# The attention's queries are turned behind the second and fourth piece of the gates in every group

## The chip, the cores and the metric

The kernel runs on one core of one Trainium2 chip. The metric is the device time of one execution in microseconds (us). Three executions of the kernel before took 1663.3 to 1664.22 us, with a median of 1663.74 us. Durations in the text come from one further execution that was profiled; it took 1663.35 us, of which 1661.6 us lie between its first and its last recorded instruction (the span).

A core has four computing engines that run side by side, each with its own queue of instructions: TensorE (PE in the profile: matrix products and transposes, with its weight loads as PEld), VectorE (DVE), ScalarE (ACT) and GpSimd (POOL). SyncE (SP) issues the DMAs that load the weights. TensorE writes its results into PSUM, which has eight banks of 128 x 512 numbers of 32 bits; ScalarE and VectorE read them from there.

## The reference

The reference is one block of a network with two branches over 256 tokens of width 2048, with 256 more tokens of context. What matters here is the attention branch:

```
xn = rmsnorm(x) * (1 + scale) + shift                     # 256 x 2048, likewise cn from the context
aq, ak, av, ag, ... = split_columns(xn @ w_in)            # w_in: 2048 x 19456
q = axial_rope(aq) * 128 ** -0.5                          # 16 heads of 128, 4 key heads
s = [q . k of the window (|i - j| <= 128), q . k of the context]
p = softmax over [s, sink]
att_branch = (p @ [v, v_ctx]) * silu(ag)
...
y = sigmoid(ma + b0) * (hg_branch @ w_o_hgrn) + sigmoid(mb + b1) * (att_branch @ w_o_attn)
out = rmsnorm(x + gate * (y @ w_out))
```

The other branch (`hg_branch`) is a gated linear recurrence in both directions. It is finished before the attention begins.

## The kernel before

All products are made from numbers split into a high and a low part (`h` and `lo`, of the type fp32r), with three matmuls for each pair of tiles (`mm3`: high x high, high x low, low x high). So each chunk of 128 x 1024 weights that a DMA has brought (`raw`) goes through ScalarE, which copies the high part (`wh`, L75), and through VectorE, which subtracts it (`wl`, L76). There are three buffers for each of `wh` and `wl` and four for `raw`. The projections write into four PSUM banks of the pool "pj"; four more banks with names of their own ("tp", "o", "al1", "al2") serve everything else.

The attention works in four groups of four heads. For group j, the generator `group_in(j, st)` makes the queries (`proj_tok_g`, eight chunks, two banks `bq`, one for each half t of the tokens) and then the gates (`proj_col_x_g`, two halves `hf` of four chunks each). A chunk of gates is called a piece in this text; it is 16 matmuls, of L140 and L145. Pieces have the numbers 0 to 7 (`4 * hf + k0 // 4`), and "step s" is the place in the program behind piece s.

A half t of the queries has two parts in `turn_q(t)`. The first is the rotation by position (`rope`, VectorE: L877, two L882, L885), from the bank into `qr`, with `rt` beside it. The second is the turn: four transposes on TensorE (L923) into `tkq`, a tile in the bank "o"; a scaled copy by ScalarE for the high part (L925); and one VectorE instruction for the low part (L926). Both write `qTa`. The table `TURNS[j][t]` says behind which step the turn of half t stands. The rope of half 0 stands ahead of piece 0, that of half 1 behind it.

When a half of the gates is finished, each of its two banks is reduced (`halves_sum`: ScalarE copies one half into `hsum`, L154, VectorE adds the other, L155); then come a sigmoid on ScalarE (L945) and a product on VectorE (L946), into `ga`. The tiles `qr`, `rt`, `hsum` and `br` (below) share two buffers, those of the tag "bb" in the pool `base`.

The generator `attend(sts)` works on 32 pairs n of a head and a half of the tokens, eight for each group. `scores(n)` makes three matmuls into the bank `sc` (L82 to L84) and then the softmax: VectorE masks, takes the maximum and its negative (L960 to L962), ScalarE takes the exponential and scales the result (L964, L965, L968), VectorE adds and inverts the sum (L966, L967). `turned(n)` transposes the probabilities of a pair (L978, `tkp`, bank "tp") and splits them (L857, L858) into `pT`. `values(m)` makes twelve matmuls for four heads into `oba`, a tile in the bank "o" (the same bank as `tkq`), and VectorE multiplies the result by the gates into `br` (L988), from which the split tiles `bH` and `bL` are made.

`alternate(attend(sts), fill(sts), 1)` weaves the two generators. `fill` runs groups 1 to 3 and then two chunks of another projection, and each `yield` of one hands over to the other. For one n the program therefore has: `scores(n)`, one chunk of `fill`, then `values(n // 4 - 1)` where n is 6, 10, 14 and so on, `turned(n - 2)`, and another chunk of `fill`. Group 0 is made before any scores, woven with the transposes of the keys.

In this part the order of TensorE's instructions is the order of the program (`tc.manual_schedule(engines={PE})`). The orders of ScalarE's, VectorE's, GpSimd's and SyncE's queues are set by a planner that simulates the program in time and gives each engine, when it comes free, the ready instruction with the highest priority; within one priority the earlier one in the program goes first. `tc.high_priority(x)` raises the priority of what is issued inside it: the splits of weights have `PRIO`, `scores`, `turned` and `values` have `2 * PRIO`, and the evictions of a turn have none.

The places of the turns, counted in `values`: in groups 1 and 3 step 3 is followed by piece 4, then by a `values` and a `turned`, and then by step 4. In group 2 it is the same: `values(2)` stands between pieces 4 and 5.

Of the kernel before, what the change touches and what calls it, by code (L numbers as in the profile page):

```python
# [7 lines left out]
F32 = mybir.dt.float32  # L8
F32R = mybir.dt.float32r
U8 = mybir.dt.uint8  # L10
AF = mybir.ActivationFunctionType
ALU = mybir.AluOpType
# [6 lines left out]
HD = 128  # L19
EPS = 1e-6  # L20
NEG = -3.0e38
PRIO = 100000
# [15 lines left out]
def block_kernel(ctx: ExitStack, tc: tile.TileContext, x, c, cx, c_ctx, w_ada, b_ada, norm_gain, w_in,  # L38
                 b_merge, lb_f, lb_b, hg_gain, w_oh, sink, w_oa, w_out, fin_gain, cst, msk, out):
    nc = tc.nc  # L40
    pe, act, dve, pool = nc.tensor, nc.scalar, nc.vector, nc.gpsimd
# [47 lines left out]
    def proj_tok_g(w, col0, src, toks):  # L89


        banks = [bank() for _ in toks]
        for k0 in range(0, KT, 2):
            h, lo = wchunk(w, k0 * P, 2, col0, 512)
            for i, t in enumerate(toks):
                for j in range(2):
                    mm3(banks[i], src(k0 + j, t), (h[:, j, :], lo[:, j, :]), k0 + j == 0, k0 + j == KT - 1)
            yield len(toks) * 6 * 512
        return banks

    def result(g):

        while True:
            try:
                next(g)
            except StopIteration as e:
                return e.value
# [21 lines left out]
    def proj_col_x_g(w, col0):  # L129

        banks = [bank() for _ in range(2)]
        for k0 in range(0, KT, 4):
            h, lo = wchunk(w, k0 * P, 4, col0, 256)
            for i in range(2):
                cs_ = slice(i * P, (i + 1) * P)
                for j in range(4):
                    kt = k0 + j

                    def both():
                        pe.matmul(banks[i].rearrange("p (a t) -> p a t", a=2), h[:, j, cs_], xHL[:, :, kt, :T],  # L140
                                  start=kt == 0, stop=kt == KT - 1)

                    if kt == 0:
                        both()
                    pe.matmul(banks[i][:, :T], lo[:, j, cs_], xH[:, kt, :T], start=False, stop=False)  # L145
                    if kt:
                        both()
            yield 24 * T
        return banks

    def halves_sum(bank_, tag, bufs):

        o = base.tile([P, 512], F32, tag=tag, name="hsum", bufs=bufs)
        act.activation(o[:, :T], bank_[:, T:], AF.Copy)  # L154
        dve.tensor_tensor(o[:, :T], bank_[:, :T], o[:, :T], op=ALU.add)  # L155
        return o[:, :T]
# [707 lines left out]
    def gt_tile(j, shape, name):  # L864
        po, tg = G_TAGS[j % 2]
        return po.tile(shape, F32, tag=tg, name=name)
# [3 lines left out]
    with tc.manual_schedule(engines={mybir.EngineType.PE}):  # L870
# [3 lines left out]
        def rope(dst, src, t):  # L874

            cos = cs[:, K_COS + t * HD: K_COS + (t + 1) * HD].unsqueeze(1).to_broadcast([P, 4, HD])
            dve.tensor_tensor(dst, src.rearrange("p (h d) -> p h d", h=4), cos, op=ALU.mult)  # L877
            tmp = base.tile([P, 4, 2, 2, 32], F32, tag="bb", name="rt", bufs=2)
            sv = src.rearrange("p (h a s d) -> p h a s d", h=4, a=2, s=2)
            sn = cs[:, K_SIN + t * HD: K_SIN + (t + 1) * HD].rearrange("p (a s d) -> p a s d", a=2, s=2)  # L880
            for s in range(2):
                dve.tensor_tensor(tmp[:, :, :, s, :], sv[:, :, :, 1 - s, :],  # L882
                                  sn[:, :, s, :].unsqueeze(1).to_broadcast([P, 4, 2, 32]), op=ALU.mult)
            tf = tmp.rearrange("p h a s d -> p h (a s d)")
            dve.tensor_tensor(dst, dst, tf, op=ALU.add)  # L885
# [21 lines left out]
                split(dst[0], dst[1], tk.rearrange("p (j t) -> p j t", j=4))  # L907
                yield

        TURNS = ((1, 3), (1, 4), (0, 3), (2, 4))

        def group_in(j, st):

            bq = yield from proj_tok_g(w_in, C_Q + 512 * j, x_st, range(2))
            def turn_q(t):
                qr = base.tile([P, 4, HD], F32, tag="bb", name="qr", bufs=2)
                rope(qr, bq[t], t)
                yield  # L920
                tk = ps.tile([P, 512], F32, tag="o", name="tkq")
                for i in range(4):
                    pe.transpose(tk[:, i * P: (i + 1) * P], qr[:, i, :], ident)  # L923
                qh, ql = [X[:, t].rearrange("p h t -> p (h t)") for X in st["q"]]
                act.activation(qh, tk, AF.Copy, scale=HD ** -0.5)  # L925
                dve.scalar_tensor_tensor(ql, tk, HD ** -0.5, qh.bitcast(F32), op0=ALU.mult, op1=ALU.subtract)  # L926

            turning = [turn_q(t) for t in range(2)]
            next(turning[0])
            st["q"] = [at.tile([P, 2, 4, P], F32R, tag=tg, name="qTa") for tg in Q_TAGS[j % 2]]  # L930
            st["g"] = gt_tile(j, [P, 4, T], "ga")
            for hf in range(2):
                bg = proj_col_x_g(w_in, C_G + 512 * j + 256 * hf)
                for k0 in range(0, KT, 4):
                    next(bg)
                    yield
                    if (hf, k0) == (0, 0):
                        next(turning[1])
                    for t in range(2):
                        if 4 * hf + k0 // 4 == TURNS[j][t]:  # L940
                            next(turning[t], None)
                for i, b in enumerate(result(bg)):
                    gs = halves_sum(b, "bb", 2)
                    gi = st["g"][:, 2 * hf + i, :]
                    act.activation(gi, gs, AF.Sigmoid)  # L945
                    dve.tensor_tensor(gi, gi, gs, op=ALU.mult)  # L946
# [61 lines left out]
        def fill(sts):  # L1008
            for j in range(1, 4):
                yield from group_in(j, sts[j])  # L1010
            yield from gates_b(0)
            sg0 = gt_tile(0, [P, 2, 512], "sgb")
            merge_gate(sgb[0], 0, 1, sg0)
            sgb[0] = sg0
            yield from gates_b(1)

        sts = [{} for _ in range(4)]
        alternate(keys(), group_in(0, sts[0]), 2)
        alternate(attend(sts), fill(sts), 1)

# [77 lines left out]
    for t in range(2):  # L1098
# [7 lines left out]
        for c0, c1, on_act in ((0, 512, True), (512, 1024, False), (1024, 1536, True), (1536, D, False)):  # L1106
# [3 lines left out]
            else:  # L1110
                e = min(c1, D - 256)
                dve.tensor_scalar(xv[t][:, c0: e], xv[t][:, c0: e], rs, None, op0=ALU.mult)
                if e < c1:
                    dve.scalar_tensor_tensor(xv[t][:, e: c1], xv[t][:, e: c1], rs, fg[1][:, e - 1024: c1 - 1024],
                                             op0=ALU.mult, op1=ALU.mult)
# [54 lines left out]
```

## Time and profile before

| | |
|---|---|
| time, median of three executions | 1663.74 us |
| the profiled execution, time / span | 1663.35 / 1661.6 us |
| TensorE busy | 1631.7 us, 98% |
| VectorE busy | 968.2 us, 58% |
| ScalarE busy | 744.7 us, 45% |
| DMA | 275.22 MB, 166 GB/s on average |
| TensorE's mean granted clock | 0.995 of full speed |
| first and last scores | at 1178.9 and 1418.8 us of the span |

Lines of the profile have different forms. In the answers about waits, a row names who waited and for whom, and then the total in us, the number of times, and the longest. In the order of time, a row has the start and the length in us, the engine, the line of the kernel, the operation, what it writes and reads, the shapes, and a count (`x4`: four instructions merged); brackets at its end hold the time that the engine stood idle before it and whose work ended that. In the rows by stretch stand the stretch, its length, the busy time and the number of instructions of PE, PEld, DVE, ACT and POOL, the granted TensorE clock (1.00 is full speed), the share of the DMA engines that were busy, and GB/s. A line "..." stands where rows are left out. Matmuls overlap, so that the distance of two starts is what one of them costs.

### The profile page before, as it was taken

Reading aid. Unit: us, or ns where it says so; the run is one execution under the profiler, and the core shown is the slowest. Engines: PE = TensorE matmul, PEld = TensorE weight load, DVE = VectorE, ACT = ScalarE, POOL = GpSimd, SP = SyncE. Lnnn points to the kernel's source line nnn. Section 1 sums busy time; section 2 is a strip of 40 time slices with the busy share of each in tenths; the row PEclk is TensorE's granted clock in tenths of the full one; section 3 lists DMA queues with packets and bytes.
Section 4 is the critical chain, followed back from the end, with each engine's and each line's share of the span. In section 5 each row is a group of like instructions: output and inputs, shape, how many; then the busy total and the mean of one; then the engine's idle time right before and its main releaser. Section 6 shows DMA issues by size and latency. Waiting matters only on the chain.

```text
span 1661.6 us, 22807 instructions
## 1 busy us (share of the span) xinstructions
PE 1631.7 (98%) x8889; PEld 1346.9 (81%) x8889; DVE 968.2 (58%) x1503; ACT 744.7 (45%) x1133; POOL 34.8 (2%) x88
## 2 busy tenths in 40 slices
PE   7999999999999999999999999999999999999998
PEld 4558888888888888888888888888878878888887
DVE  4444577546665466745677455325667667555665
ACT  4333444324442344423455443224676767444443
POOL 2000000000000000000000000000000000000000
PEclk9999999999999999999999999999999999999999
DMA  9993444346343553435445556334534445665554
GB/s 354 381 386 108 151 141 140 102 135 191 93 126 116 161 169 102 129 113 176 105 129 171 182 190 194 123 102 145 173 119 149 131 144 159 213 215 190 188 191 140
DMA packets 191436, 275.22 MB, mean 166 GB/s; under 512 B 9808, under 2 KB 112480, under 8 KB 190560
## 3 DMA queue, kind: packets, MB, share of 16 engines
q1 hardware_dynamic: 189344, 269.39, 50.9%
q0 software_dynamic: 1264, 3.25, 1.0%
q8 instruction: 70, 1.15, 0.3%
q10 hardware_dynamic: 720, 1.11, 0.2%
q14 instruction: 38, 0.31, 0.1%
HBM read 271.61 MB, written 2.11 MB: 165 GB/s over the span
## 4 chain that ended last, share of the span: by engine, by line
PE 94%; DMA 3%; ACT 1%; DVE 1%; issue 1%; POOLq 0%; POOL 0%; SPq 0%; ACTq 0%
PE pj L82 23%; PE pj L84 23%; PE pj L83 23%; PE pj L140 7%; PE pj L145 4%; DMA raw<-in_w_ada_dram 3%; PE al L559 2%; PE pa L304 1%; PE pj L394 1%; PE sb L636 1%; PE tkp L978 1%; PE pj L387 1%; PE pj L388 1%; DMA X<-in_x_dram 0%; PE ob L677 0%
## 5 line engine op out<-in xcount | busy, mean ns | idle before, releaser
L76 DVE TENSOR_TENSOR wl<-raw,wh 128x1024 fp32r<-128x1024 f32 x392 | 479.3, 1223 | 432.4 <-ACT wh L75 431.9
L75 ACT ACTIVATE wh<-raw 128x1024 fp32r<-128x1024 f32 x392 | 414.8, 1058 | 590.6 <-PE pj L84 419.5
L83 PE MATMUL pj<-wl,xHL 128*128 128x512 f32 (+1 forms) x1024 | 395.5, 386 | 0.4 <-DVE wl L76 0.4
L84 PE MATMUL pj<-wh,xHL 128*128 128x512 f32 (+1 forms) x1024 | 395.4, 386 | 0.0
L82 PE MATMUL pj<-wh,xHL 128*128 128x512 f32 (+1 forms) x1024 | 391.0, 390 | 0.0
L84 PEld LDWEIGHTS pj<-wh,xHL 128*128 128x128 f32 x1024 | 192.4, 188 | 39.1
L83 PEld LDWEIGHTS pj<-wl,xHL 128*128 128x128 f32 x1024 | 192.5, 188 | 38.2 <-DVE wl L76 0.7
L82 PEld LDWEIGHTS pj<-wh,xHL 128*128 128x128 f32 x1024 | 192.2, 188 | 38.0 <-DVE yt L1034 0.4
L140 PE MATMUL pj<-xHL,wh 128*128 128x512 f32 x512 | 183.3, 400 | 0.0
L82 PE MATMUL pj<-xHL,wh 128*128 128x512 f32 x416 | 164.3, 395 | 0.0
L84 PE MATMUL pj<-xHL,wl 128*128 128x512 f32 x416 | 162.1, 390 | 0.0
L83 PE MATMUL pj<-xHL,wh 128*128 128x512 f32 x416 | 162.0, 390 | 0.0
L145 PE MATMUL pj<-xHL,wl 128*128 128x256 f32 x512 | 140.7, 285 | 0.0
L140 PEld LDWEIGHTS pj<-xHL,wh 128*128 128x128 f32 x512 | 96.4, 191 | 20.4
L145 PEld LDWEIGHTS pj<-xHL,wl 128*128 128x128 f32 x512 | 98.1, 192 | 2.7
L83 PE MATMUL pj<-wl,bH 128*128 128x512 f32 x256 | 99.9, 390 | 0.0
L84 PE MATMUL pj<-wh,bL 128*128 128x512 f32 x256 | 99.7, 389 | 0.0
L84 PEld LDWEIGHTS pj<-xHL,wl 128*128 128x128 f32 x416 | 78.1, 188 | 16.4
L83 PEld LDWEIGHTS pj<-xHL,wh 128*128 128x128 f32 x416 | 78.2, 188 | 15.5
L82 PEld LDWEIGHTS pj<-xHL,wh 128*128 128x128 f32 x416 | 78.2, 188 | 15.6
L82 PE MATMUL pj<-wh,bH 128*128 128x512 f32 x256 | 89.9, 390 | 0.1
L602 DVE TENSOR_TENSOR A<-A,X 128x512 f32<-128x512 f32 x96 | 62.0, 688 | 15.9 <-ACT so L536 6.1
(272 smaller groups left out, 1737.9 us busy)
## 6 DMA issues: line engine op xcount, KB each, us to landing
raw<-in_w_in_dram SPq DMA_DIRECT2D x292, 512.0 KB, 3.6
raw<-in_w_ada_dram SPq DMA_DIRECT2D x128, 256.0 KB, 5.5
raw<-in_w_ada_dram SPq DMA_DIRECT2D x32, 512.0 KB, 3.8
raw<-in_w_o_hgrn_dram SPq DMA_DIRECT2D x32, 512.0 KB, 3.7
raw<-in_w_o_attn_dram SPq DMA_DIRECT2D x32, 512.0 KB, 3.9
raw<-in_w_out_dram SPq DMA_DIRECT2D x32, 512.0 KB, 4.4
raw<-in_w_in_dram SPq DMA_DIRECT2D x24, 256.0 KB, 5.4
X<-in_x_dram SPq DMA_DIRECT2D x2, 1024.0 KB, 6.4
```

Of the source, the lines that this page charges most:

```text
L75: act.activation(h[:, :n], raw[:, :n], AF.Copy)
L76: dve.tensor_tensor(lo[:, :n], raw[:, :n], h[:, :n].bitcast(F32), op=ALU.subtract)
L82: pe.matmul(o, s[0], m[0], start=first, stop=False)
L83: pe.matmul(o, s[0], m[1], start=False, stop=False)
L84: pe.matmul(o, s[1], m[0], start=False, stop=last)
L140: pe.matmul(banks[i].rearrange("p (a t) -> p a t", a=2), h[:, j, cs_], xHL[:, :, kt, :T], start=kt == 0, stop=kt == KT - 1)
L145: pe.matmul(banks[i][:, :T], lo[:, j, cs_], xH[:, kt, :T], start=False, stop=False)
L304: pe.matmul(pa[32 * g: 32 * g + 32, : 2 * w], cT[:, k0 + g, :], rv_[:, :, g % nk, :], start=k0 == 0, stop=k0 == KT - 4, tile_position=(0, ...
L387: pe.matmul(o, hw, xH[:, kt, :], start=kt == 0, stop=False)
L388: pe.matmul(o, lo[:, kt - k, cs_], xH[:, kt, :], start=False, stop=False)
L559: pe.matmul(o, ky, mv, start=True, stop=True, tile_position=(0, 64 * c))
L602: dve.tensor_tensor(av, av, f.unsqueeze(3).to_broadcast([P, 2, n2, b]), op=ALU.mult)
```

## The change

The table `TURNS` goes away. In every group, half 0 is turned behind piece 1 (the second) and half 1 behind piece 3 (the fourth). The tile `tkq` stays in the bank "o". The two evictions of a turn get the priority `2 * PRIO`.

```diff
-        TURNS = ((1, 3), (1, 4), (0, 3), (2, 4))
...
-                act.activation(qh, tk, AF.Copy, scale=HD ** -0.5)
-                dve.scalar_tensor_tensor(ql, tk, HD ** -0.5, qh.bitcast(F32), op0=ALU.mult, op1=ALU.subtract)
+                with tc.high_priority(2 * PRIO):
+                    act.activation(qh, tk, AF.Copy, scale=HD ** -0.5)
+                    dve.scalar_tensor_tensor(ql, tk, HD ** -0.5, qh.bitcast(F32), op0=ALU.mult, op1=ALU.subtract)
...
-                    for t in range(2):
-                        if 4 * hf + k0 // 4 == TURNS[j][t]:
-                            next(turning[t], None)
+                    if hf == 0 and k0 in (4, 12):
+                        next(turning[k0 // 8], None)
```

## The prediction

> **What bounds the kernel now.** I read the page first, then who TensorE waited for over the whole span, then the three places that this table points to in order of time, and last the granted clock around them.
>
> ```profile
> span 1661.6 us, 22807 instructions
> ...
> PE 1631.7 (98%) x8889; PEld 1346.9 (81%) x8889; DVE 968.2 (58%) x1503; ACT 744.7 (45%) x1133; POOL 34.8 (2%) x88
> ...
> PE tkq L923 <- DVE br L988: 8.3, 2, 4.1
> PE tk L282 <- DMA cs<-in_const_dram: 6.2, 1, 6.2
> PE idle L408 <- DVE cols L255: 2.2, 1, 2.2
> ...
> PE oba L82 <- DVE qTa L926: 0.8, 1, 0.8
> ...
> PE pj L83 <- DVE wl L76: 0.4, 1, 0.4
> ```
>
> TensorE is busy for 98% of the span: time is won only where it stands still or runs slowly. The largest entry of the waits (total, times, longest) is the turning of queries, `tkq`, which waited twice for 4.1 us until VectorE had read the values' result out of the bank that both use. Both are of a second turn put behind the fifth piece, `TURNS[j][1] == 4`, in groups 1 and 3: there the order on TensorE is scores, piece, `values`, `turned`, turn. Group 1:
>
> ```profile
> 1218.94 0.39 PE L140 MATMUL pj<-xHL,wh 128*128 128x512 f32 x1
> ...
> 1221.74 0.39 PE L82 MATMUL oba<-pT,xHL 128*128 128x512 f32 x1
> ...
> 1224.49 0.60 PE L978 MATMUL tkp<-cs,pr 128*128 128x128 f32 x4
> 1229.22 0.94 PE L923 MATMUL tkq<-cs,qr 128*128 128x128 f32 x4 [4.13 <-DVE br L988]
> ...
> 1230.17 0.63 PE L140 MATMUL pj<-xHL,wh 128*128 128x512 f32 x1
> ...
> 1230.81 0.63 PE L140 MATMUL pj<-xHL,wh 128*128 128x512 f32 x1
> ...
> 1232.73 0.45 PE L140 MATMUL pj<-xHL,wh 128*128 128x512 f32 x1
> ...
> 1225.56 1.28 ACT L945 ACT_TABLE_LOAD   x1
> 1226.85 0.42 ACT L945 ACTIVATE ga<-hsum 128x256 f32<-128x256 f32 x1
> ...
> 1227.30 0.43 DVE L946 TENSOR_TENSOR ga<-ga,hsum 128x256 f32<-128x256 f32 x1 [1.37 <-ACT ga L945]
> ...
> 1228.39 0.68 DVE L988 TENSOR_TENSOR br<-oba,ga 128x512 f32<-128x512 f32 x1
> ```
>
> The first column is the start, the second the length. `values` is issued by 1224.49, but its reader `br` begins only at 1228.39, behind the second half-sum's sigmoid (1226.85) and product (1227.30): `qr`, `rt`, `hsum` and `br` share the two buffers of tag "bb", and the second `qr` holds one until its turn. So it is a ring: the turn waits for `br`, and `br` for a gate that has to squeeze through the other buffer. After the wait a pair of gate matmuls takes 0.64 us (1230.17 to 1230.81). Group 3, the clock, and the normal pace in group 2:
>
> ```profile
> 1350.85 0.60 PE L978 MATMUL tkp<-cs,pr 128*128 128x128 f32 x4
> 1355.58 0.99 PE L923 MATMUL tkq<-cs,qr 128*128 128x128 f32 x4 [4.13 <-DVE br L988]
> ...
> 1359.14 0.40 PE L140 MATMUL pj<-xHL,wh 128*128 128x512 f32 x1
> ...
> 1231.00:1233.00 2.00, 2.00 (x8) 1.67 (x7) 0.51 (x1) 0.00 (x0) 0.00 (x0) 0.55 0.00 0
> 1233.00:1235.00 2.00, 2.00 (x12) 1.73 (x11) 0.06 (x1) 0.75 (x1) 0.00 (x0) 1.00 0.00 0
> ...
> 1291.58 0.60 PE L978 MATMUL tkp<-cs,pr 128*128 128x128 f32 x4
> 1291.94 0.36 PE L145 MATMUL pj<-xHL,wl 128*128 128x256 f32 x1
> 1292.14 0.39 PE L140 MATMUL pj<-xHL,wh 128*128 128x512 f32 x1
> ...
> 1292.49 0.40 PE L140 MATMUL pj<-xHL,wh 128*128 128x512 f32 x1
> ```
>
> In the stretches of 2 us, third from the end is the granted clock: 0.55 behind the wait, then 1.00. Undisturbed, four transposes take 0.36, the next matmul 0.20, each pair 0.35 us.
>
> **The change part by part.** Nothing is added or removed on any engine; a turn is four transposes and two evictions, and issues no DMA; all is order. `TURNS` was ((1,3), (1,4), (0,3), (2,4)), and every group now has (1,3).
>
> *Group 0*: its steps stay. Only the priority of its two evictions is new. Nobody waits on them in the table above. 0, and no gain is possible.
>
> *Second turn of groups 1 and 3, from step 4 to step 3*: now the order is scores, turn, piece, `values`. The bank's last user is then the first turn, two pieces back (7.1 us: 1211.80 below, 1218.94), so the second finds it free. What goes, by group: the wait, from 1224.49 + 0.36 = 1224.85 to 1229.22, 4.37 us; in group 3 from 1350.85 + 0.36 = 1351.21 to 1355.58, 4.37 us. And the slow stretch: `tkq`, one L145 and four pairs should take 0.36 + 0.20 + 4 x 0.35 = 1.96 us, and took 1232.73 - 1229.22 = 3.51 and 1359.14 - 1355.58 = 3.56: 1.55 and 1.60 us. Sum 11.9 us. The transposes themselves only change places.
>
> [...]
>
> *What is late next*: `values`, one piece later, needs the bank back from the turn's two evictions, ScalarE's `qh` and VectorE's `ql`. Group 2 has this order already:
>
> ```profile
> 1284.56 0.60 PE L923 MATMUL tkq<-cs,qr 128*128 128x128 f32 x4
> ...
> 1287.56 0.40 PE L140 MATMUL pj<-xHL,wh 128*128 128x512 f32 x1
> 1288.72 0.50 PE L82 MATMUL oba<-pT,xHL 128*128 128x512 f32 x1 [0.76 <-DVE qTa L926]
> ...
> 1285.13 1.28 ACT L945 ACT_TABLE_LOAD   x1
> 1286.42 0.42 ACT L945 ACTIVATE ga<-hsum 128x256 f32<-128x256 f32 x1
> 1286.75 0.71 ACT L968 ACTIVATE pr<-pr,mx 128x512 f32<-128x512 f32 x1
> 1287.36 0.58 ACT L925 ACTIVATE qTa<-tkq 128x512 fp32r<-128x512 f32 x1
> ...
> 1287.97 0.69 DVE L926 SCALAR_TENSOR_TENSOR qTa<-tkq,qTa 128x512 fp32r<-128x512 f32 x1 [0.67 <-ACT qTa L925]
> ...
> 1220.81 0.42 ACT L945 ACTIVATE ga<-hsum 128x256 f32<-128x256 f32 x1
> ```
>
> There the next matmul could follow at 1287.56 + 0.23 = 1287.79 and came at 1288.72: 0.93 us, with the eviction behind a table load, a sigmoid and a scaling of scores. In group 1 the new turn begins at 1218.94, `values` is due 0.36 + 2.80 later, at 1222.1. If the order on ScalarE stays (last row: the sigmoid of the first half, now at 1220.81), `qh` runs from 1221.2 to 1221.8, `ql` to 1222.5: a wait of 0.4 us. If the new priority puts `qh` ahead of the sigmoid and the table load in front of it (1.28 us, as in group 2), it runs from 1219.6, and `ql` is done before 1222.1 even behind a weight split of 1.2 us: no wait. Bounds 0 and 0.93 for each group; I take 0.45 for groups 1 and 3, since the priority can only overtake the sigmoid if the planner sees the turn finished when ScalarE comes free, and group 2 shows it did not. Group 2 itself goes from 0.93 to something between 0 and 0.93; I take 0.7.
>
> *First turns, group 2 from step 0 to 1 and group 3 from step 2 to 1*: no wait stands before either now, and the bank is free. What depends on them is the second rope, whose `rt` takes the buffer that the first turn frees:
>
> ```profile
> 1342.02 0.76 DVE L882 TENSOR_TENSOR rt<-pj,cs 128x256 f32<-128x256 f32 x2 [0.55 <-PE tkq L923]
> ...
> 1273.88 0.64 PE L923 MATMUL tkq<-cs,qr 128*128 128x128 f32 x4
> ...
> 1211.80 0.60 PE L923 MATMUL tkq<-cs,qr 128*128 128x128 f32 x4
> ...
> 1215.52 0.68 DVE L885 TENSOR_TENSOR qr<-qr,rt 128x512 f32<-128x512 f32 x1
> ```
>
> In group 1, whose first turn is at step 1 already, the rope ends at 1216.20, 4.4 us behind the turn (1211.80), and the new slot is 1218.94: 2.7 us to spare. In group 2 the first turn moves some 4 us, from 1273.88 to about 1278, so its rope would end near 1282.3, against a slot at 1284.56. In group 3 the step earlier helps. 0 for all; if the cover of 2.3 us went, the excess would be paid one to one.
>
> *The priority*: `qh` and `ql` (0.58 and 0.69 us) may now overtake weight splits. Weights stand three chunks ahead, 2.8 us each, and no TensorE wait on `wl` exceeds the 0.4 of the table: 0, bounded by 0.4 either way.
>
> *Sum*, against the profiled execution (1663.35 us; span 1661.6): -11.9 + 2 x 0.45 - (0.93 - 0.7) = -11.2, so 1652.1. The median of the runs, 1663.74, stands 0.4 higher; I give 1652.4.
>
> **The rivals.** *A, the values' wait takes over.* ScalarE could meet one more switch of tables and an exponential before `qh`, 1.28 + 0.69 = 2.0 us beyond the bound, in each of three groups. Then the waits are 3 x 2.9 = 8.8 in place of 0.93, the gain 11.9 - 7.9 = 4.0, the time 1659.5; with half of it, 1655.6. For it: group 1's ScalarE loads a table once more at 1225.56. Against it: `qh` now has the scores' own priority. [...]
>
> *B, slower than before.* `qh` falls behind both gates' sigmoids, as `br` does now: in group 1 to about 1227.2, `ql` to 1228.5, a wait of 6.4 us, and 1.55 for the clock. Three groups: 23.9 - 0.93 - 11.9 = +11: 1674.5. It decides from (11.9 + 0.93) / 3 = 4.3 us of wait and slow clock per group. Against it: the second sigmoid waits in group 1 for a buffer that the earlier turn now frees, and in group 2 `qh` went ahead of it.
>
> *C, the plan shifts.* ScalarE's, VectorE's and SyncE's orders come from the planner's simulated time, so everything behind the first new priority may be dealt out anew; one new wait of a size seen here (2.2 to 4.4 us with its clock) takes the time to 1654.5 to 1658.5.
>
> *D, nothing measurable.* The ring could close on the other turn, if a rope is late by what is won. Two waits of 4 us would have to arise; the cover of 2.3 us speaks against it: 1660.5 to 1667.
>
> **How the numbers follow.** Forecast 0.73 (1650.6 to 1653.9: all three waits 0, or all 0.93 and a little); A 0.11; C 0.09; D 0.04; B 0.03. The range from 1650.4 to 1656.0 takes the forecast, and the near halves of A and C: some 0.82. A measurement here tells about 0.2%, 3.3 us, from no change. Faster: the forecast, C and nearly all of A, 0.92; the same 0.05; slower 0.03.
>
> **What would show it.** The row of `tkq` waiting for `br` is gone, and the granted clock stays at 1.00 in the attention; `oba` waiting for `qTa` stands three times at up to 0.9 us; `br` comes within 2 us of the last `oba`. A wrong prediction would show `oba` rows of over 2 us (A, B), `tkq` waiting for `qr` (D), or a name that is new in the table of waits (C).

## The result

The changed kernel takes 1652.01 us (median of six executions, 1651.65 to 1653.84) against 1663.66 us (median of six). The ratio of the means, here and below, is 0.9933, with a 95% interval of 0.992 to 0.9945. Forecast were 1652.4 us and a range of 1650.4 to 1656.0. Two of the six executions took 1653.33 and 1653.84 us; ten later ones of the same kernel, told below, all lie between 1651.46 and 1652.17. No trace of the two slower ones exists, so what they waited for stays open. The profiled execution took 1651.65 us, 11.70 us less than the one of before.

The head of the page after, and who TensorE waited for over the whole span (total us, times, longest):

```profile
span 1649.9 us, 22804 instructions
## 1 busy us (share of the span) xinstructions
PE 1628.7 (99%) x8889; PEld 1343.6 (81%) x8889; DVE 968.0 (59%) x1503; ACT 746.7 (45%) x1135; POOL 34.4 (2%) x88
```

```profile
PE tk L282 <- DMA cs<-in_const_dram: 6.1, 1, 6.1
PE idle L408 <- DVE cols L255: 2.3, 1, 2.3
...
PE oba L82 <- DVE qTa L923: 0.3, 2, 0.2
```

The row of 8.3 us, `tkq` behind `br`, is gone, and no turn waits for anything. What stood below it is unchanged. TensorE has the same 8889 matmuls, but 3.0 us less of busy time (1628.7 against 1631.7): that is about what the slow stretches lost, since they count as busy. The same three stretches of the span, which hold groups 1, 2 and 3, before and then after (the changed kernel is further on in its work in the later ones); the columns are length, the busy time of PE, PEld, DVE, ACT and POOL, the granted clock, the DMA share and GB/s:

```profile
1179.00:1244.00 65.00, 60.87 (x308) 51.51 (x307) 43.73 (x86) 44.41 (x73) 0.00 (x0) 0.97 0.44 133
1244.00:1312.00 68.00, 67.24 (x350) 56.58 (x348) 50.56 (x100) 48.91 (x84) 0.00 (x0) 1.00 0.47 144
1312.00:1372.00 60.00, 55.87 (x288) 47.37 (x287) 40.03 (x77) 40.47 (x66) 0.00 (x0) 0.97 0.46 142
```

```profile
1179.00:1244.00 65.00, 64.85 (x333) 54.61 (x332) 47.83 (x95) 49.70 (x82) 0.00 (x0) 1.00 0.50 152
1244.00:1312.00 68.00, 67.85 (x351) 57.09 (x350) 50.70 (x97) 49.68 (x83) 0.00 (x0) 1.00 0.46 141
1312.00:1372.00 60.00, 59.85 (x313) 50.48 (x312) 44.48 (x87) 44.90 (x74) 0.60 (x1) 1.00 0.52 161
```

Groups 1 and 3 had a mean clock of 0.97 and stood idle for 4.1 us each; now the clock is 1.00, and each of the three groups has 0.15 us of idle time. In order of time, group 1 on TensorE, and the `values` of groups 2 and 3:

```profile
1218.80 0.60 PE L919 MATMUL tkq<-cs,qr 128*128 128x128 f32 x4
1219.16 0.47 PE L140 MATMUL pj<-xHL,wh 128*128 128x512 f32 x1
...
1221.80 0.40 PE L140 MATMUL pj<-xHL,wh 128*128 128x512 f32 x1
1222.34 0.50 PE L82 MATMUL oba<-pT,xHL 128*128 128x512 f32 x1
...
1282.47 0.50 PE L82 MATMUL oba<-pT,xHL 128*128 128x512 f32 x1 [0.15 <-DVE qTa L923]
...
1342.59 0.50 PE L82 MATMUL oba<-pT,xHL 128*128 128x512 f32 x1 [0.15 <-DVE qTa L923]
```

`values` was due 0.23 us behind 1221.80, at 1222.03, and came 0.31 us later, with a first matmul that costs 0.34 in place of 0.23 us. Groups 2 and 3 show the same: their last matmuls of the gates begin at 1281.92 and 1342.04, so both come 0.32 us late. ScalarE's and VectorE's queues in group 1 show why:

```profile
1219.37 1.28 ACT L941 ACT_TABLE_LOAD   x1
1220.66 0.42 ACT L941 ACTIVATE ga<-hsum 128x256 f32<-128x256 f32 x1
1220.99 0.58 ACT L922 ACTIVATE qTa<-tkq 128x512 fp32r<-128x512 f32 x1
1221.46 0.37 ACT L154 ACTIVATE hsum<-pj 128x256 f32<-128x256 f32 x1
...
1221.60 0.69 DVE L923 SCALAR_TENSOR_TENSOR qTa<-tkq,qTa 128x512 fp32r<-128x512 f32 x1
...
1226.83 0.43 DVE L942 TENSOR_TENSOR ga<-ga,hsum 128x256 f32<-128x256 f32 x1 [0.50 <-ACT ga L941]
1227.17 0.68 DVE L984 TENSOR_TENSOR br<-oba,ga 128x512 f32<-128x512 f32 x1
```

The eviction stands behind the table load and the sigmoid, as in the first of the two cases that were worked out, and ends at 1222.29. `br` begins at 1227.17, still 4.8 us behind the start of `values` and directly behind the product of the second half-sum, but nobody needs the bank by then. The last matmul of `values` begins at 1224.99 and ends 0.40 us later, so `br` comes 1.8 us behind it (3.7 us before the change: 1224.25 + 0.40 and 1228.39). The second `qr` is read by then, so it is not what holds `br` here; what does is not shown.

### The profile page after: what moved, and what is told of

It reads as the page before. It is cut to its first block, busy times and chain, and to the rows that moved or that the text cites. A ratio compares the mean times of both kernels' runs of the same rounds, so it can differ in the third digit from the quotient of the medians.

```text
span 1649.9 us, 22804 instructions
## 1 busy us (share of the span) xinstructions
PE 1628.7 (99%) x8889; PEld 1343.6 (81%) x8889; DVE 968.0 (59%) x1503; ACT 746.7 (45%) x1135; POOL 34.4 (2%) x88
## 4 chain that ended last, share of the span: by engine, by line
PE 95%; DMA 2%; DVE 1%; ACT 1%; issue 1%; SPq 0%; POOLq 0%; POOL 0%; ACTq 0%
PE pj L82 23%; PE pj L83 23%; PE pj L84 23%; PE pj L140 7%; PE pj L145 3%; PE al L559 2%; PE pa L304 2%; PE pj L394 1%; DMA raw<-in_w_ada_dram 1%; PE pj L387 1%; PE sb L636 1%; PE tkp L974 1%; PE pj L388 1%; DMA X<-in_ctx_dram 1%; DVE wl L76 1%
```

## The experiments

The theory: each second turn directly behind `values` costs 4.4 us of wait and a stretch of slow clock, because `br` reads the common bank late; what counts is the distance of a second turn from `values`, and nothing else in the change matters. The rivals: the priority does part of it; the first turns do; the wait belongs to something else in groups 1 and 3, or would move to another place.

Times are medians. The kernel before, run beside each set on the same chip, took 1663.53 us beside the parts of the change, 1663.65 beside the next four kernels and 1663.95 beside the last four.

**The parts of the change.** First the changed kernel itself, as a mark:

> The changed kernel itself, as the mark for the others on the same chip. Both theories: 1651.7 to 1653.8 us, 11 to 12 us under the kernel before; TensorE waits for the turn's evictions ahead of `values` three times, about 0.3 us each, and never in front of a turn.

1651.87 us (1651.46 to 1652.17). Then the steps without the priority:

```diff
-        TURNS = ((1, 3), (1, 4), (0, 3), (2, 4))
+        TURNS = ((1, 3), (1, 3), (1, 3), (1, 3))
```

> The new steps in every group, without the new priority. Theory (the place of the second turns is all of it): within 0.5 us of the changed kernel, about 1652 us, and the eviction stands in ScalarE's queue where it stood with the priority, behind the table load and the sigmoid. Rival (the priority keeps the wait of `values` short): each of three waits at 0.9 us or more in place of 0.32, so 1653.9 us or more.

1651.96 us (1651.83 to 1652.14), and on each of the five engines the instructions stand in the same order as in the changed kernel. The priority alone, on the old steps:

```diff
+                with tc.high_priority(2 * PRIO):
                     act.activation(qh, tk, ...)
                     dve.scalar_tensor_tensor(ql, tk, ...)
```

> The new priority with the old steps. Theory: 1663.7 us, both 4.1 us waits of `tkq` for `br` stay. Rival (the priority does part of the work): 1 us or more under the kernel before.

1663.69 us, a ratio of 1.0002 (0.9992 to 1.0011), again with every queue in the order of the kernel before, and with its waits:

```profile
PE tkq L923 <- DVE br L989: 8.3, 2, 4.1
PE oba L82 <- DVE qTa L927: 0.8, 1, 0.8
```

So the priority does nothing here, in either kernel. By its rule the planner gives an engine that comes free the best of what is ready, so wherever it chose, the eviction was not yet ready, or without a rival that the priority reverses; which of the two is not shown. Next the second turns alone:

```diff
+        TURNS = ((1, 3), (1, 3), (0, 3), (2, 3))
```

> Only the second turns of groups 1 and 3 move from step 4 to step 3; the first turns stay at steps 1, 0 and 2, and there is no new priority. Theory: nearly all of the gain, 11.9 us less at most 0.6 us for each of two waits that are longer than in the changed kernel: 1651.7 to 1653.2 us. Rival (the moves of the first turns carry a part, since they free the buffer for the second rope): group 3's second turn waits for its `qr` by up to 1 us, and the time is 1653 to 1654 us.

1652.38 us (1652.26 to 1652.86): 11.15 of the 11.66 us that the whole change brought beside it. Who TensorE waited for in the attention of this kernel:

```profile
PE oba L82 <- DVE qTa L926: 0.9, 2, 0.8
PE pj L83 <- DVE wl L76: 0.4, 1, 0.4
PE tkq L923 <- DVE qTa L926: 0.4, 1, 0.4
```

Group 2's `values` still waits 0.8 us, since its first turn at step 0 leaves a scaling of scores ahead of the eviction. Group 3's second turn now waits 0.4 us for the low part of the first, which at step 2 is only one piece ahead in the same bank. The moves of the first turns are thus worth 0.4 us between the medians of the two kernels without the priority (1652.38 and 1651.96), and 0.9 us in their profiled executions, where the stretch from the first scores to the last takes 229.17 and 228.29 us. They act through the bank and not through the `qr` that the rival named.

**One wait, and three.** Only group 1:

```diff
+        TURNS = ((1, 3), (1, 3), (0, 3), (2, 4))
```

> Only group 1's second turn moves, from step 4 to step 3; group 3 keeps step 4. Theory (each of the two waits has its own price, 4.37 us of wait and 1.6 us of slow clock): half of the gain less 0.3 us for the new wait of `values`, 5.6 us, so 1657.9 us. Rival (one wait takes the other's place, so that the first that goes is found again later): 1661 us or more, with a longer wait in group 3.

1658.51 us, 5.1 us less where 5.6 were expected, and group 3 waits 4.1 us as before: each wait has its own price, and none takes the other's place. The 0.5 us that is missing stands in the clock of group 3, in stretches of 2 us of this kernel (third from the end):

```profile
1349.00:1351.00 2.00, 0.84 (x5) 0.87 (x5) 1.30 (x3) 0.93 (x2) 0.00 (x0) 0.50 0.00 0
1351.00:1353.00 2.00, 2.00 (x9) 1.71 (x8) 1.09 (x2) 0.60 (x1) 0.00 (x0) 0.50 0.03 8
1353.00:1355.00 2.00, 2.00 (x9) 1.72 (x8) 0.00 (x0) 0.00 (x0) 0.00 (x0) 0.53 0.00 0
1355.00:1357.00 2.00, 2.00 (x13) 1.70 (x12) 0.50 (x2) 1.06 (x1) 0.00 (x0) 1.00 0.00 0
```

Behind the same wait, the matmuls are slow from the turn at 1350.16 to 1355.00, for 4.8 us in place of 3.6. And the other way, with group 2 also behind `values`:

```diff
+        TURNS = ((1, 3), (1, 4), (0, 4), (2, 4))
```

> The other way: group 2's second turn also goes behind `values`, to step 4, as in groups 1 and 3 before. Theory: a third wait of 4.4 us and 1.6 us of slow clock, less the 0.93 us that group 2's `values` waits for no longer: 1663.5 + 5.0 = 1668.5 us. Rival (the wait in groups 1 and 3 comes from something of theirs, such as their buffers for the gates): group 2 waits under 2 us, and the time is 1665 us or less.

1668.99 us, ratio 1.003 (1.0018 to 1.0042), 5.3 us over the kernel before. Its waits in the attention, and the clock behind the third wait in group 2:

```profile
PE tkq L923 <- DVE br L988: 12.4, 3, 4.2
```

```profile
1294.00:1296.00 2.00, 1.58 (x7) 1.51 (x8) 0.97 (x2) 1.08 (x2) 0.00 (x0) 0.50 0.00 0
1296.00:1298.00 2.00, 2.00 (x8) 1.71 (x7) 0.69 (x1) 0.14 (x1) 0.00 (x0) 0.50 0.00 0
1298.00:1300.00 2.00, 2.00 (x8) 1.71 (x7) 0.00 (x0) 0.00 (x0) 0.00 (x0) 0.50 0.00 0
1300.00:1302.00 2.00, 2.00 (x11) 1.74 (x11) 0.72 (x2) 1.06 (x1) 0.00 (x0) 0.94 0.00 0
```

Three waits of 4.1 us where there were two: the price belongs to the place behind `values`, not to groups 1 and 3. In this execution the slow stretch of group 2 cost 2.7 us, where 1.6 were expected.

**Why `br` is late.** The steps of before, but the half-sums of the gates take their buffer elsewhere:

```diff
-                    gs = halves_sum(b, "bb", 2)
+                    gs = halves_sum(b, "sm", 3)
```

> The steps of before, but `hsum` of the gates takes its buffer from the tag "sm" (three buffers, shared with the probabilities) and not from "bb". Theory (the ring through the buffers of "bb" makes `br` late): `br` starts within 1 us of the last matmul of `values`, the two waits shrink to 1 us or so, the clock stays at 1.00, and the time is 1653 to 1655 us. Rival (ScalarE and VectorE are too full there, with table loads and the split of the probabilities ahead of `br`): waits of over 3 us stay, and 1660 us or more.

1652.6 us, ratio 0.9933 (0.9918 to 0.9947), with the second turns of groups 1 and 3 still at step 4, and a little under the 1653 to 1655 us expected. VectorE and TensorE in group 1:

```profile
1224.65 0.69 DVE L988 TENSOR_TENSOR br<-oba,ga 128x512 f32<-128x512 f32 x1
...
1225.40 0.66 PE L923 MATMUL tkq<-cs,qr 128*128 128x128 f32 x4 [0.34 <-DVE br L988]
```

`br` begins at 1224.65, directly behind `values`, in place of 1228.39. With its buffer no longer tied to the gates, the wait of 4.13 us is 0.34 us in group 1 and 0.35 us in group 3, and the granted clock stays at 1.00 in the three groups. One new wait came: the first turn of group 2, at step 0, waits 0.7 us for its rope.

```profile
PE tkq L923 <- DVE qr L885: 0.7, 1, 0.7
PE tkq L923 <- DVE br L988: 0.7, 2, 0.3
```

Taken alone, this run does not tell the ring from the rival of too much work, because the half-sums now wait for the probabilities' buffers and come later themselves: the table load ahead of the gates' first sigmoid is at 1226.99, behind `br`. ScalarE's and VectorE's rows of the kernel before in group 1 tell more:

```profile
1222.90 0.36 ACT L154 ACTIVATE hsum<-pj 128x256 f32<-128x256 f32 x1
...
1225.57 0.16 DVE L966 TENSOR_TENSOR mx<-mx 128x1 f32<-128x1 f32 x1 [0.98 <-ACT mx L965]
...
1227.30 0.43 DVE L946 TENSOR_TENSOR ga<-ga,hsum 128x256 f32<-128x256 f32 x1 [1.37 <-ACT ga L945]
```

The result of `values` was complete at 1224.25 + 0.40 = 1224.65. From then on VectorE stood idle for 0.92 us and again for 1.37 us, room enough for the 0.68 us of `br`. But the second half-sum held one buffer of "bb" from 1222.90 to the end of its product at 1227.73, and the second `qr` held the other until its turn at 1229.22. So `br` had no buffer, and VectorE was not too full. ScalarE, though, had no gap from 1222.90 to the sigmoid at 1226.85: the ring makes `br` wait for the gate, and ScalarE's queue makes the gate late. What each of the two is worth alone is not shown.

**The distance alone.** Later in place of earlier, two pieces behind step 4:

```diff
+        TURNS = ((1, 3), (1, 6), (0, 6), (2, 6))
```

> The second turn later in place of earlier: step 6 in groups 1 to 3, behind `values` and two further pieces; first turns and priority as before. Theory (only the distance from `values` counts): `br` is late as before, but read 2 us ahead of the turn; no wait before the turn, none before `values`: 1650.7 to 1651.3 us. Rival (the second `qr` keeps its buffer of "bb" for longer, and the ring closes elsewhere): a new wait of TensorE behind step 6, 1653 us or more.

1650.76 us (1650.47 to 1650.88). `br` is as late as ever, but the turn comes 2.6 us behind its end (1228.51 + 0.68 = 1229.19). VectorE, then TensorE, in group 1 of this kernel:

```profile
1228.51 0.68 DVE L988 TENSOR_TENSOR br<-oba,ga 128x512 f32<-128x512 f32 x1
```

```profile
1231.77 0.60 PE L923 MATMUL tkq<-cs,qr 128*128 128x128 f32 x4
```

TensorE was busy for all of 193.00 us in the three stretches of groups 1 to 3. It was then put beside the changed kernel on one chip, with a place between the two, and with one still earlier:

> The changed kernel again, as the mark for the next three on one chip: 1651.5 to 1652.2 us in most runs, three waits of 0.3 us ahead of `values`.

> The kernel with the second turns behind the seventh piece (step 6) again, beside the changed kernel on one chip. Theory (what is left between them are the three waits ahead of `values`, 0.32 us and 0.11 us of a slower first matmul each): 1.1 to 1.3 us under the changed kernel. Rival (the difference was that of two chips): within 0.4 us of it.

1651.84 us (1651.56 to 1651.97) and 1650.78 us (1650.48 to 1651.32): 1.06 us apart, a little under the 1.1 to 1.3 expected from three waits.

```diff
+        TURNS = ((1, 3), (1, 5), (0, 5), (2, 5))
```

> The second turns of groups 1 to 3 behind the sixth piece (step 5), one piece and one pair's scores, 3.4 to 3.5 us, later than step 4. Theory (`br` comes at a fixed time, some 4.4 us behind the last transposes of `turned`, and only the rest is waited for): waits of 0.9 us before each of three turns, the clock stays at 1.00, and the time is about 3 us over step 6: 1653.8 us. Rival (a turn so near behind `values` moves `br` itself back, since the turn's rope holds the buffer): waits of 2 us or more, and over 1657 us.

1653.76 us (1653.23 to 1654.1), where 1653.8 were expected. TensorE and VectorE in group 1:

```profile
1229.19 0.39 PE L84 MATMUL sc<-xHL,qTa 128*128 128x512 f32 x1
1230.23 0.63 PE L923 MATMUL tkq<-cs,qr 128*128 128x128 f32 x4 [0.66 <-DVE br L988]
```

```profile
1229.41 0.68 DVE L988 TENSOR_TENSOR br<-oba,ga 128x512 f32<-128x512 f32 x1
```

`br` keeps its time: it begins 3.92 us behind the transposes of `turned` (1225.49), against 3.90 us in the kernel before (1224.49 and 1228.39). The turn was due 0.23 us behind 1229.19 and came 0.81 us later. Three such waits, with a clock of 1.00, are 2.4 of the 2.98 us over step 6, so that the median met the expectation is in part luck. In the profiled executions of the two kernels (1654.1 and 1650.81 us), 0.8 us of the difference stands ahead of the attention, where no turn was moved: the first scores begin at 1179.95 and at 1179.14 us. Last, both turns a step earlier than in the change:

```diff
+        TURNS = ((0, 2), (0, 2), (0, 2), (0, 2))
```

> Both turns one step earlier than in the changed kernel, behind the first and the third piece, in every group, without the new priority. Theory (an earlier second turn gives `values` its bank in time, and a first turn behind one piece finds its `qr` ready): no wait ahead of `values`, 1650.8 us, at most 0.5 us more where a first turn is just late. Rival (the cover of the ropes is used up): waits of TensorE for `qr` in front of the turns, 0.5 us or more in several groups, and 1652 us or more.

1650.64 us (1650.55 to 1650.79), ratio 0.992 (0.9906 to 0.9933), with no TensorE wait in groups 1 to 3: an earlier turn gives `values` its bank in time, and the ropes' cover was not used up. This and step 6 are the best versions here, 1.1 to 1.2 us under the changed kernel on the same chip (medians, with ranges that do not meet). Both are at the end of this mechanism: no wait of a turn or of `values` is left to take.

## Why the prediction was right, point by point

**What bounds.** TensorE's stops were the time to be won, and the two rows named were the ones that went. The three groups without a wait (step 6) and the whole ladder of places, 1668.99 for three turns directly behind `values`, 1653.76 one piece later, 1650.78 two pieces later (the first on another chip than the others), carry the reading that the distance decides.

**The two waits: 4.37 us each, right.** With the slow clock the terms were 11.89 us; the pair that begins at 1232.73 in group 1 took 0.40 in place of 0.35 us as well, which makes 11.94.

**The slow clock: 1.55 and 1.60 us, right for that execution, but not a constant.** Against the normal pace (0.56 us for the turn and one matmul, 0.35 us for a pair), the stretch costs 1.10 + 3.74 - 0.56 - 2.10 = 2.2 us in group 3 of the kernel with one wait, and in the kernel with three, 1.4, 2.7 and 1.6 us. That both terms were near 1.6 us in the execution that the prediction read is luck; on this step it should have had a range and not a point. The last section shows what the loss goes by. The 0.55 that the prediction quotes is the mean of a stretch of 2 us; the granted clock itself was 0.50. In the traces the clock was at 0.50 for 3.41 us in groups 1 and 3 before, and for at least 6.7 us in the cases that lost 2.2 and 2.7 us, and it fell at different points of waits of equal length (last section).

**The wait of `values`: mis-sized.** I put 0.45, 0.45 and 0.7 us, and all three were 0.32 (0.31 in group 1), because with the first turn moved group 2 has the order of group 1, with no scaling of scores between the sigmoid and the eviction. I left out that the first matmul behind each wait costs 0.11 us more. With both, the sum is 11.94 + (0.93 + 0.11) - 3 x (0.32 + 0.11) = 11.69 us, and the profiled executions differ by 11.70, of which 11.60 lie between the first and the last scores (1178.94 to 1418.85 us before, 1178.79 to 1407.10 after). The prediction's own sum of 11.2 was 0.5 us short.

**The first turns: "0 for all" was wrong by 0.4 to 0.9 us.** I looked only at the rope behind them. With the second turns at step 3, group 3's first turn at step 2 would have kept the bank from its second one: the wait of 0.4 us that the second turns alone show.

**The priority: 0, right, for a weaker reason than the true one.** I bounded a shift of the weight splits; in fact no engine's order changes.

**The rivals.** A and B needed the eviction behind more of ScalarE's work; it went directly behind the first sigmoid, and the second half-sum found its buffer free at 1221.46, as the prediction held against B. C did not come about: no new row stands in the waits. D did not either: at step 3 no turn waits for its rope. The 1.28 us that A reckons for a table load are what one took after the change too, with its sigmoid 0.01 us behind it (1219.37 + 1.28, sigmoid at 1220.66).

## What to carry to other kernels

Where two users share one bank, read what stands between the first one's last write and its reader, and put the second user ahead of the first or far enough behind; one piece more or less was worth 5 us here, and the direction mattered little. A late reader need not be slow itself: look for the buffer that it waits for, and who holds that one. Here the ring opened at either of two links, the place of the turn and the buffer of the gates. A priority changed no queue here: before you count on one, see whether two instructions are ready at once where it should decide.

## What was not expected of the hardware

Behind waits of the same length, 4.13 to 4.16 us by the profile, TensorE's matmuls ran at a granted clock of 0.50 for anything from 3.0 us (1228.99 to 1232.00 in the kernel with three waits) to 5.8 us (from 1294.42 in the same execution). The clock in finer stretches: one low stretch of the kernel before, then that of the kernel with one wait, then the long one of the kernel with three:

```profile
1229.45:1232.80 3.35, 3.35 (x14) 2.96 (x13) 1.38 (x2) 0.89 (x2) 0.00 (x0) 0.50 0.00 0
...
1348.10:1354.80 6.70, 4.64 (x16) 4.18 (x17) 3.10 (x5) 2.43 (x5) 0.00 (x0) 0.50 0.02 8
...
1293.45:1300.25 6.80, 5.83 (x20) 5.18 (x21) 2.21 (x4) 1.34 (x3) 0.00 (x0) 0.50 0.00 0
```

The low stretch of group 3 before, 1355.70 to 1359.11, is as long as that of group 1, 1229.41 to 1232.82: 3.41 us. The other two that are shown last at least 6.70 and 6.80 us. For groups 1 and 3 of the kernel with three waits the mean clock is 0.97, as for the same groups of the kernel before. The clock did not fall at the same point of the wait: in group 1 before, 0.2 us behind the start of the turn (1229.41 and 1229.22), and with one wait left, 2.06 us or more ahead of it (0.50 from 1348.10 on, the turn at 1350.16). There it was low 2.1 us behind the end of the last transposes (1345.43 + 0.60 = 1346.03); in group 1 before, it fell 4.3 us behind theirs (1224.49 + 0.60 = 1225.09). What set these points is not shown. TensorE has nothing to run inside the wait, so what counted here is how much of the low stretch the matmuls met: 3.0 to 3.4 us cost 1.4 to 1.6 us, 4.7 us cost 2.2, and 5.8 us cost 2.7. Waits of 0.34 us (group 1 with the half-sums' buffer elsewhere) to 0.76 us (group 2 before) left the mean clock of their groups at 1.00.
